# The beginning of a decoder step: weights staged in idle tiles, one weight split on another engine, small products between the first steps

## The chip, the cores and the metric

The kernel runs on one core of a Trainium2 chip. The metric is the device time of one execution in microseconds (us); lower is better. The engines are named as in the profile: PE (TensorE, the matrix products), DVE (VectorE), ACT (ScalarE), POOL (GpSimd) and SP (SyncE, which here only issues transfers).

## The reference, cut to what matters

One inference step of a decoder with two layers, for 512 prompt rows and 8 single-token samples, all float32, 1024 features wide. Only the first sublayer, windowed attention, is touched by the change:

```python
def qkv_proj(x, w_qkv, b_qkv, offset):
    qkv = x @ w_qkv + b_qkv
    q = qkv[..., :nq].reshape(B, T, N_HEADS, HEAD_DIM)
    k = qkv[..., nq:nq + nk].reshape(B, T, N_KV_HEADS, HEAD_DIM)
    v = qkv[..., nq + nk:].reshape(B, T, N_KV_HEADS, HEAD_DIM)
    return rope(q, pos), rope(k, pos), v
...
scores = jnp.einsum('bnqkgd,bnskd->bnkgqs', qb, kk) * ATTN_SCALE
probs = sink_softmax(scores, mask, sink)
o = jnp.einsum('bnkgqs,bnskd->bnqkgd', probs, vv) @ w_o
x = layer_norm(ALPHA * x + o)
```

After it come a gated feed-forward sublayer with a short convolution, then gated linear attention with four heads (a matrix state that is carried along the rows, and one more state for each sample), and a second feed-forward sublayer. Caches, states and the last convolution rows are outputs too.

## The kernel before, in words

**Rows and groups.** Activations lie with the features on the 128 partitions, as 8 chunks of 128 features (KD = 8). The rows are in two groups: a (256 prompt rows) and b (the other 256 and the 8 samples, 264 columns). A name ending in _a or _b belongs to that group.

**Products in three parts.** A float32 product is made from float32r products: every operand is split into a high part (a copy to float32r: wh of a weight, xh of x) and a low part (the rest: wl, xl), and three products are added up in one bank of PSUM: wh x xh, wh x xl, wl x xh. In group a, xh and xl lie in one tile, xs_a. `product` (L224) does this for one *unit*, a weight of 1024 x 128: 8 steps over the feature chunks, 24 matmuls; L236, L238 and L240 are the three products of a step. Where its flag `behind` (L230) is set, all eight wl products come after the others.

**Units.** Unit 0 gives the keys (`attn_k`, L575), unit 1 the values (`attn_v`), units 2 to 9 the queries of two heads each (`attn_q`, L610). Each is used twice, for group a and then for group b, three units later at the start (LAG - 1).

**Loading a weight** (`load_unit`, L180). SP's queue brings the weight into a tile `raw`, of which there are two (RAWS = 2); ACT (L194) or, for the units below HIACT, POOL (L196) makes wh, and DVE makes wl (L200). Six pairs of wh and wl are held (WSLOTS = 6). A transfer into `raw` waits until DVE has read what lay there two units earlier, and everything behind it on SP's queue waits too.

**The beginning** (`attn_open`, L514). PE first multiplies a tile of ones with itself, 8 times (L524 to L526; WARM = 8), into a bank that nobody reads. SP's queue, whose order is written out by hand, brings: unit 0 and x of group a in alternating pieces, unit 1 in four pieces, parameters, rope table and identity, unit 2 in two pieces, unit 3 in one, x of group b (x_b) in two pieces, the rest of the tables, and units 4 and 5. Group b's x is split by ACT (L313, xh_b) and DVE (L314, xl_b).

**Keys.** After unit 0, `rope` (L561) turns the keys with ACT, DVE and POOL into rr, and `attn_k` splits them: four copies by ACT (khi, L583 and L584) and four differences by DVE (klo, L586 and L587), since each half is kept on both halves of the partitions. The scores (L650, L651) take khi, klo and the queries' parts qs, which travel from the tile hl by small transfers (L622).

**Caches.** The samples' key and value caches, kc and vc, are two tiles of 128 x 1024. Transfers fill them late, while group b's queries are made (L631, L633).

**What sets the order.** Python code emits the work unit by unit, interleaving groups, with later parts of a head's work put on a list with a delay. From this a scheduler with a timing model of its own orders each engine's instructions, before the program is built; `issue_after(x)` keeps what follows behind instruction x, and only SP's queue at the beginning is fixed. So an edit at the beginning may reorder instructions much later.

**Linear attention**, which the prediction also speaks of: in each head the samples' states are updated on DVE from a tile vb (L1185) that a transfer fills for two samples at a time; only one vb exists. A gate tile sg is multiplied out of a PSUM bank (L1210), attm is a masked copy (L1073), dmn belongs to the next head's decay (L1025), and three transposes (L1090 to L1092) go into the bank that sg has been read from.

Of the kernel before, what the change touches and what calls it, by code (L numbers as in the profile page):

```python
# [11 lines left out]
F32 = mybir.dt.float32  # L12
F32R = mybir.dt.float32r
I32 = mybir.dt.int32
AF = mybir.ActivationFunctionType
ALU = mybir.AluOpType
# [4 lines left out]
P = 128  # L21
D = 1024
KD = 8
SEQ = 512
NS = 8
# [15 lines left out]
LAG = 4  # L41
# [1 line left out]

WSLOTS = 6
RAWS = 2
HIACT = 2

PAIRED = 4
ORDERED = 3
# [11 lines left out]
LOWS = 7  # L61
# [24 lines left out]
def in_turn(rows):  # L86

    return rows.rearrange("p t j -> p j t")
# [10 lines left out]
class Net:  # L99
# [77 lines left out]
        return self.acc.tile([P, 2, 512], F32, name=f"widep{i}")  # L177


    def load_unit(self, u, pieces=1, late=False):  # L180
        src, nt = self.units[u][0], self.units[u][1]
        nc = self.nc
        if nt == 0:
            return self.load_rank(u)
        r = self.raw.tile([P, KD * P], F32, name="raw")
        h, l = ((self.wx if u == self.extra else self.wts).tile([P, KD * P], F32R, name=name) for name in ("wh", "wl"))
        n = nt * P // pieces
        for c in (slice(i * n, (i + 1) * n) for i in range(pieces)):
            nc.sync.dma_start(out=r[:, c], in_=src[:, c])
            if late:  # L190
                self.spawn(self.parts(u, h[:, c], l[:, c], r[:, c], src[:, c]), 1)
                continue
            if u >= HIACT:
                nc.scalar.activation(h[:, c], r[:, c], AF.Copy)  # L194
            else:
                nc.gpsimd.tensor_scalar(h[:, c], r[:, c], 1.0, 0.0, op0=ALU.mult, op1=ALU.add)  # L196
            if self.units[u][2] in (self.ffn_down2, self.ffn_gate, self.ffn_value):
                self.low_by_dma(l[:, c], h[:, c], src[:, c])
            else:
                nc.vector.tensor_tensor(l[:, c], r[:, c], h[:, c].bitcast(F32), op=ALU.subtract)  # L200
        self.w[u] = (h, l)
# [22 lines left out]
    def product(self, g, u, rh, rl):  # L224
        nc = self.nc
        h, l = self.w[u]
        nt = self.units[u][1]

        tail = u in self.phases[2::3] or g.i and u in self.phases[2:4]
        behind = self.units[u][2] == self.ffn_down and g.i == 0 or g.i == 0 and nt == KD and not tail and any(e < u < e + LOWS for e in (*self.phases[2:4], *self.phases[5:6]))  # L230
        ps = self.acc.tile([P, 512], F32, name="accp")
        o = ps[:, :g.n].rearrange("p (j t) -> p j t", t=2)
        for k in range(nt):
            ks = slice(k * P, (k + 1) * P)
            xh, xl = in_turn(rh[:, k]), in_turn(rl[:, k])
            nc.tensor.matmul(o, h[:, ks], xh, start=k == 0, stop=False)  # L236
            if not tail:
                nc.tensor.matmul(o, h[:, ks], xl, start=False, stop=False)  # L238
            if not behind:
                nc.tensor.matmul(o, l[:, ks], xh, start=False, stop=not tail and k == nt - 1)  # L240
        for k in range(nt) if tail or behind else ():
            w, r = (h, rl) if tail else (l, rh)
            nc.tensor.matmul(o, w[:, k * P:(k + 1) * P], in_turn(r[:, k]), start=False, stop=k == nt - 1)
        self.final = self.nc.cur_bb.bb.instructions[-1]
        return ps[:, :g.n]
# [268 lines left out]
    def attn_open(self):  # L514
        nc, I = self.nc, self.I
        self.ap, self.ap_cm = self.open("attn")
        p = self.ap
        t = lambda s, name, dt=F32: p.tile(s, dt, name=name)
        self.rope_t = t([P, 2, NT], "rope_t")
        self.mask0 = t([P, P], "mask0")  # L520
        self.own = t([P, 2, P], "own", I32)


        warm = self.acc.tile([P, 512], F32, name="accp")  # L524
        for _ in range(WARM):
            nc.tensor.matmul(warm[:, :P], self.ones_a, self.ones_a, start=True, stop=True)  # L526
        with self.tc.manual_schedule(engines={mybir.EngineType.SP}):
            r = self.raw.tile([P, KD * P], F32, name="raw")
            h, l = (self.wts.tile([P, KD * P], F32R, name=n) for n in ("wh", "wl"))
            for m in range(0, KD, 4):  # L530
                c = slice(m * P, m * P + 4 * P)
                nc.sync.dma_start(out=r[:, c], in_=I["w_qkv"][0][:, c])
                nc.gpsimd.tensor_scalar(h[:, c], r[:, c], 1.0, 0.0, op0=ALU.mult, op1=ALU.add)
                self.load_x(0, m, m + 2)
                nc.vector.tensor_tensor(l[:, c], r[:, c], h[:, c].bitcast(F32), op=ALU.subtract)
                self.load_x(0, m + 2, m + 4)
            self.w[0] = (h, l)
            self.load_unit(1, 4)
            nc.sync.dma_start(out=self.par, in_=I["par"])
            nc.sync.dma_start(out=self.rope_t[:, :, 0:256], in_=I["rope"][:, :, 0:256])  # L540
            nc.sync.dma_start(out=self.ident, in_=I["ident"])
            self.load_unit(2, 2)
            self.load_unit(3)
            for m in range(0, KD, 4):
                self.load_x(1, m, m + 4)
            nc.sync.dma_start(out=self.rope_t[:, :, 256:], in_=I["rope"][:, :, 256:])
            nc.sync.dma_start(out=self.mask0, in_=I["mask"])
            nc.sync.dma_start(out=self.own, in_=I["own"])
            for i in range(4, WSLOTS):
                self.load_unit(i)  # L550
        self.bq = t([P, KD], "bq")
        nc.vector.tensor_scalar(self.bq, self.par[:, C_BQKV + 2:C_BQKV + 10], 0.125, None, op0=ALU.mult)
        self.khi = [t([P, SEQ], f"khi{v}", F32R) for v in range(2)]
        self.klo = [t([P, SEQ], f"klo{v}", F32R) for v in range(2)]
        self.vtok = t([P, 4, P], "vtok")
        self.kc = t([P, NS, P], "kc")
        self.vc = t([P, NS, P], "vc")
        self.qz = t([P, NS * P], "qz")
        nc.gpsimd.memset(self.qz, 0.0)

# [14 lines left out]
    def attn_k(self, g, u):  # L575
        nc = self.nc
        ps = self.product(g, u, g.xh, g.xl)
        r = self.rope(g, ps, 1.0, self.par[:, C_BQKV:C_BQKV + 1])
        cs = slice(g.c0, g.c0 + 256)
        for v in range(2):  # L580
            own = slice(64 * v, 64 * v + 64)
            oth = slice(64 - 64 * v, 128 - 64 * v)
            nc.scalar.activation(self.khi[v][own, cs], r[own, :256], AF.Copy)  # L583
            nc.scalar.activation(self.khi[v][oth, cs], r[own, :256], AF.Copy)  # L584
            hi = self.khi[v][own, cs].bitcast(F32)
            nc.vector.tensor_tensor(self.klo[v][own, cs], r[own, :256], hi, op=ALU.subtract)  # L586
            nc.vector.tensor_tensor(self.klo[v][oth, cs], r[own, :256], hi, op=ALU.subtract)  # L587
        yield 0
        if g.i:
            self.pcopy(self.kc[:, :, 127], r[:, 256:])  # L590
            nc.scalar.dma_start(out=self.O["k_prompt"], in_=r[:, 128:256])
# [901 lines left out]
```

## Time and profile before

| | |
|---|---|
| median of 3 executions | 1099.32 us (1099.08 to 1100.93) |
| the profiled execution's time, and its span | 1098.55 us, 1096.6 us |
| busy, share of the span: PE, DVE, ACT, POOL | 97%, 80%, 60%, 28% |
| PE busy in the first three stretches of 10 us | 8.06, 8.97, 9.58 us |
| PE's granted clock there | 0.89, 0.94, 1.00 |
| DVE busy there | 4.89, 9.26, 9.27 us |
| ACT busy there | 4.32, 7.10, 4.89 us |
| transfers there | 256, 300, 146 GB/s |

The profile is one execution seen by the hardware profiler. A row of its timeline has the start, the duration, the engine, the line, the operation, what is written and read (`out<-in`), shape, type and count, and in brackets the idle time before it with what ended it. A row of stretches has from:to, the length, each engine's busy time with its number of instructions in brackets, and last the granted clock of PE (1.00 is full speed), the busy share of the transfer engines and GB/s. Groups of rows that follow each other closely are merged into one with a count. Some records of matmuls can be missing.

### The profile page before, as it was taken

What the parts mean: (1) busy time and instruction counts of PE and PEld (TensorE: products, weight loads), DVE (VectorE), ACT (ScalarE), POOL (GpSimd) and SP (SyncE); (2) the same over time, 40 slices, a digit from 0 to 9 for tenths busy, and PEclk for the clock granted to TensorE, in tenths of its full rate; (3) what the DMA queues carried; (4) which work ended last, traced back from release to release, by engine and by line L of the source; (5) the groups of instructions that cost most, each with busy time, mean ns of one, the idle gap of its engine ahead of it and who ended that gap; (6) DMA issues with size and microseconds to landing.
All of it is one profiled execution on the core that took longest, in us unless ns stands there. A gap on an engine that the chain in (4) does not pass through costs nothing.

```text
span 1096.6 us, 23781 instructions
## 1 busy us (share of the span) xinstructions
PE 1058.9 (97%) x9174; PEld 1031.2 (94%) x9174; DVE 882.0 (80%) x1797; ACT 663.1 (60%) x1308; POOL 303.1 (28%) x512
## 2 busy tenths in 40 slices
PE   8999999999999999999899999999999999999996
PEld 8997899999999999999799899899999999999995
DVE  7897668988778878978667678778988788888975
ACT  5677667766655665547545456458776655655643
POOL 4576562221111110274111100362221111110163
PEclk9999999999999999999999999999999999999998
DMA  7554048587777774437224364558588777774412
GB/s 233 147 173 125 21 128 207 135 215 191 180 177 178 176 174 116 124 130 204 66 74 145 115 185 136 164 170 215 134 205 197 180 174 177 175 185 116 116 66 79
DMA packets 65472, 167.44 MB, mean 153 GB/s; under 512 B 8104, under 2 KB 28624, under 8 KB 65360
## 3 DMA queue, kind: packets, MB, share of 16 engines
q1 hardware_dynamic: 50960, 119.47, 33.8%
q0 software_dynamic: 12240, 44.57, 23.1%
q10 hardware_dynamic: 2160, 1.89, 0.5%
q8 instruction: 72, 1.18, 0.4%
q14 instruction: 40, 0.33, 0.1%
HBM read 153.24 MB, written 8.47 MB: 147 GB/s over the span
## 4 chain that ended last, share of the span: by engine, by line
PE 66%; DVE 13%; DMA 10%; ACT 5%; issue 5%; SPq 1%; POOL 0%; DVEq 0%; ACTq 0%; POOLq 0%
PE widep L308 8%; PE widep L310 8%; PE widep L309 8%; PE accp L236 6%; PE accp L238 6%; PE accp L240 6%; PE widep L921 5%; PE widep L920 5%; PE widep L919 5%; DMA vb<-dv 2%; DMA wl<-in_w_up 2%; DVE wl L200 2%; PE onep L310 1%; PE onep L309 1%; PE onep L308 1%
## 5 line engine op out<-in xcount | busy, mean ns | idle before, releaser
L313 ACT ACTIVATE wh<-raw 128x1024 fp32r<-128x1024 f32 x72 | 76.2, 1061 | 98.7 <-PE widep L920 57.3
L194 ACT ACTIVATE wh<-raw 128x1024 fp32r<-128x1024 f32 (+1 forms) x92 | 96.0, 1047 | 52.3 <-PE accp L238 19.4
L309 PE MATMUL widep<-tl,wh 128*128 128x264 f32 (+1 forms) x432 | 119.1, 276 | 0.0
L310 PE MATMUL widep<-th,wl 128*128 128x264 f32 (+1 forms) x432 | 119.1, 276 | 0.0
L308 PE MATMUL widep<-th,wh 128*128 128x264 f32 (+1 forms) x432 | 119.1, 276 | 0.0
L236 PE MATMUL accp<-xh_b,wh 128*128 128x264 f32 x400 | 113.1, 283 | 2.6 <-DVE hprod L817 2.6
L240 PE MATMUL accp<-xh_b,wl 128*128 128x264 f32 x400 | 111.5, 279 | 0.0
L236 PE MATMUL accp<-xs_a,wh 128*128 128x256 f32 x400 | 106.1, 285 | 5.4 <-DVE sg L1202 2.5
L238 PE MATMUL accp<-xl_b,wh 128*128 128x264 f32 x384 | 107.5, 280 | 0.0
L206 POOL DMA_DIRECT2D wl<-in_w_down x28 | 24.3, 866 | 293.6 <-ACT wl L205 271.0
L238 PE MATMUL accp<-xs_a,wh 128*128 128x256 f32 x384 | 103.1, 284 | 0.5
L314 DVE TENSOR_TENSOR wl<-raw,wh 128x1024 fp32r<-128x1024 f32 x72 | 87.5, 1218 | 7.5 <-ACT wh L313 7.5
L205 ACT ACTIVATE wl<-wh 128x1024 fp32r<-128x1024 f32 x85 | 89.1, 1051 | 1.0
L200 DVE TENSOR_TENSOR wl<-raw,wh 128x1024 fp32r<-128x1024 f32 (+2 forms) x64 | 79.0, 1244 | 12.3 <-ACT wh L194 11.5
L236 PEld LDWEIGHTS accp<-xs_a,wh 128*128 128x128 f32 x400 | 76.7, 195 | 7.0 <-DVE sg L1202 2.9
L308 PEld LDWEIGHTS widep<-th,wh 128*128 128x128 f32 x432 | 82.1, 190 | 0.0
L309 PEld LDWEIGHTS widep<-tl,wh 128*128 128x128 f32 x432 | 82.1, 190 | 0.0
L310 PEld LDWEIGHTS widep<-th,wl 128*128 128x128 f32 x432 | 82.1, 190 | 0.0
L236 PEld LDWEIGHTS accp<-xh_b,wh 128*128 128x128 f32 x400 | 75.7, 189 | 4.3 <-DVE hprod L817 3.4
L308 PE MATMUL widep<-xh_b,wh 128*128 128x264 f32 x288 | 79.6, 276 | 0.0
L309 PE MATMUL widep<-xl_b,wh 128*128 128x264 f32 x288 | 79.5, 276 | 0.0
L310 PE MATMUL widep<-xh_b,wl 128*128 128x264 f32 x288 | 79.5, 276 | 0.0
(419 smaller groups left out, 4113.1 us busy)
## 6 DMA issues: line engine op xcount, KB each, us to landing
raw<-in_w_up SPq DMA_DIRECT2D x88, 512.0 KB, 4.0
wl<-in_w_up POOLq DMA_DIRECT2D x52, 512.0 KB, 7.1
raw<-in_w_down SPq DMA_DIRECT2D x44, 512.0 KB, 3.9
wl<-in_w_down POOLq DMA_DIRECT2D x28, 512.0 KB, 6.5
raw<-in_w_gla SPq DMA_DIRECT2D x24, 512.0 KB, 3.5
raw<-in_w_mix_o SPq DMA_DIRECT2D x16, 512.0 KB, 4.1
qs<-hl SPq DMA_DIRECT2D x64, 64.0 KB, 2.1
sgla<-in_state_gla SPq DMA_DIRECT2D x16, 256.0 KB, 2.9
```

What stands on the lines that cost most here:

```text
L194: nc.scalar.activation(h[:, c], r[:, c], AF.Copy)
L200: nc.vector.tensor_tensor(l[:, c], r[:, c], h[:, c].bitcast(F32), op=ALU.subtract)
L205: self.nc.scalar.activation(l, h.bitcast(F32), AF.Copy, scale=-1.0)
L236: nc.tensor.matmul(o, h[:, ks], xh, start=k == 0, stop=False)
L238: nc.tensor.matmul(o, h[:, ks], xl, start=False, stop=False)
L240: nc.tensor.matmul(o, l[:, ks], xh, start=False, stop=not tail and k == nt - 1)
L308: self.nc.tensor.matmul(o, h[:, ks], rh, start=k == 0, stop=False)
L309: self.nc.tensor.matmul(o, h[:, ks], rl, start=False, stop=False)
L310: self.final = self.nc.tensor.matmul(o, l[:, ks], rh, start=False, stop=k == KD // 2 - 1).ins
L313: self.nc.scalar.activation(hi, src, AF.Copy)
L314: self.nc.vector.tensor_tensor(lo, src, hi.bitcast(F32), op=ALU.subtract)
L919: nc.tensor.matmul(o, h[:, ks], rh, start=k == 0, stop=False)
```

## The change

Five edits, all for the first 25 us of the program:

- Units 2 and 3 are loaded into the tiles kc and vc, which are allocated earlier for that, each in two pieces; they no longer take a `raw` tile.
- HIACT goes from 2 to 1: wh of unit 1 is made by ACT, not by POOL.
- In group a the wl products of units 0 to 3 come behind their other products (`u < LAG`).
- Between the first eight steps of unit 0 in group a stands one product of ones with ones, seven in all, into the bank of the opening products.
- khi and klo, of both groups, stay behind the last instruction of ACT and of DVE that has been emitted when x_b's splits have been.

```diff
-HIACT = 2
+HIACT = 1
...
-    def load_unit(self, u, pieces=1, late=False):
+    def load_unit(self, u, pieces=1, late=False, r=None):
...
-        r = self.raw.tile([P, KD * P], F32, name="raw")
+        if r is None:
+            r = self.raw.tile([P, KD * P], F32, name="raw")
...
-        behind = self.units[u][2] == self.ffn_down and g.i == 0 or g.i == 0 and nt == KD and not tail and any(e < u < e + LOWS for e in (*self.phases[2:4], *self.phases[5:6]))
+        behind = self.units[u][2] == self.ffn_down and g.i == 0 or g.i == 0 and nt == KD and not tail and (u < LAG or any(e < u < e + LOWS for e in (*self.phases[2:4], *self.phases[5:6])))
...
             if not tail:
-                nc.tensor.matmul(o, h[:, ks], xl, start=False, stop=False)
+                step = nc.tensor.matmul(o, h[:, ks], xl, start=False, stop=False)
+            if u == 0 and g.i == 0 and k < nt - 1:
+                with self.tc.issue_after(step.ins):
+                    nc.tensor.matmul(self.warm[:, :P], self.ones_a, self.ones_a, start=True, stop=True)
...
-            self.load_unit(2, 2)
-            self.load_unit(3)
+            self.load_unit(2, 2, r=self.kc.rearrange("p b d -> p (b d)"))
+            self.load_unit(3, 2, r=self.vc.rearrange("p b d -> p (b d)"))
             for m in range(0, KD, 4):
                 self.load_x(1, m, m + 4)
+            self.rows = [next(x for x in reversed(nc.cur_bb.bb.instructions) if x.engine == engine)
+                         for engine in (mybir.EngineType.Activation, mybir.EngineType.DVE)]
...
-        for v in range(2):
...
+        with self.tc.issue_after(self.rows[0]), self.tc.issue_after(self.rows[1]):
+            for v in range(2):
```

Lines of the changed kernel are up to five higher than before. What the scheduler makes of it on PE at the end of unit 0 (`accp_218` before and `accp_219` now are unit 0's bank, `accp_259` and `accp_267` unit 1's, `accp_102` that of the ones), before:

```order
L236 MATMUL accp_218<-xs_a_87,wh_112 128x256
L236 MATMUL accp_259<-xs_a_87,wh_141 128x256
L238 MATMUL accp_259<-xs_a_87,wh_141 128x256
L238 MATMUL accp_218<-xs_a_87,wh_112 128x256
L240 MATMUL accp_218<-xs_a_87,wl_113 128x256
```

and now:

```order
L239 MATMUL accp_219<-xs_a_87,wh_114 128x256
L242 MATMUL accp_102<-ones_a_80 128x128
L237 MATMUL accp_219<-xs_a_87,wh_114 128x256
L237 MATMUL accp_267<-xs_a_87,wh_143 128x256
L239 MATMUL accp_267<-xs_a_87,wh_143 128x256
L237 MATMUL accp_267<-xs_a_87,wh_143 128x256
L239 MATMUL accp_267<-xs_a_87,wh_143 128x256
L239 MATMUL accp_219<-xs_a_87,wh_114 128x256
L247 MATMUL accp_219<-xs_a_87,wl_115 128x256 x8
```

A product of ones follows each of the first seven steps, four matmuls of unit 1 are drawn ahead where two were, and unit 0's eight low products stand in one row at its end.

On ACT, from unit 2's high part to unit 5's (`raw`, `kc` and `vc` are where the weight lies; `bq` marks a query unit, `par` keys or values), before:

```order
L194 ACTIVATE wh<-raw 128x512 x2
L597 ACTIVATE ra<-accp,par 128x256
L583 ACTIVATE khi_209<-rr 64x256
L584 ACTIVATE khi_209<-rr 64x256
L583 ACTIVATE khi_210<-rr 64x256
L584 ACTIVATE khi_210<-rr 64x256
L194 ACTIVATE wh<-raw 128x1024
L313 ACTIVATE xh_b<-x_b 128x264 x4
L566 ACTIVATE ra<-accp,bq 128x256
L313 ACTIVATE xh_b<-x_b 128x264 x4
L566 ACTIVATE ra<-accp,bq 128x256
L194 ACTIVATE wh<-raw 128x1024 x2
```

and now, from unit 3's second half on:

```order
L195 ACTIVATE wh<-vc 128x512
L317 ACTIVATE xh_b<-x_b 128x264 x4
L570 ACTIVATE ra<-accp,bq 128x256
L317 ACTIVATE xh_b<-x_b 128x264 x4
L588 ACTIVATE khi_212<-rr 64x256
L589 ACTIVATE khi_212<-rr 64x256
L588 ACTIVATE khi_213<-rr 64x256
L589 ACTIVATE khi_213<-rr 64x256
L570 ACTIVATE ra<-accp,bq 128x256
L195 ACTIVATE wh<-raw 128x1024
L622 ACTIVATE hl<-rr 128x256
L195 ACTIVATE wh<-raw 128x1024
```

The four khi copies moved from ahead of unit 3's high part to behind x_b's splits, ahead of the high parts of units 4 and 5, and one hl copy came in between these two.

The scheduler also reorders the rest of attention and the linear attention; in the two feed-forward sublayers the order of PE's matmuls is as it was. One place in the first linear-attention head, on DVE, where the last pair of samples is updated (L1185, now L1190), before:

```order
L1185 SCALAR_TENSOR_TENSOR sgla<-vb,kraw,sgla 128x256 x2
L1210 SCALAR_TENSOR_TENSOR sg<-tp,par,sg 128x256
L1073 COPY_PREDICATED attm_7292<-causal,sc 128x256
L1025 TENSOR_SCALAR dmn<-sc,par 128x264
L314 TENSOR_TENSOR hs_a<-sg,hs_a 128x2x128
```

and now:

```order
L1190 SCALAR_TENSOR_TENSOR sgla<-vb,kraw,sgla 128x256 x2
L1078 COPY_PREDICATED attm_7300<-causal,sc 128x256
L1030 TENSOR_SCALAR dmn<-sc,par 128x264
L1215 SCALAR_TENSOR_TENSOR sg<-tp,par,sg 128x256
L318 TENSOR_TENSOR hs_a<-sg,hs_a 128x2x128
```

The two instructions attm and dmn moved ahead of sg; PE's transposes into sg's bank come behind sg in both.

More of the change, by code (lines that the diff above doesn't have):

```diff
@@ L521, in attn_open @@
         self.own = t([P, 2, P], "own", I32)
-        warm = self.acc.tile([P, 512], F32, name="accp")
+        self.kc = t([P, NS, P], "kc")
+        self.vc = t([P, NS, P], "vc")
+        self.warm = self.acc.tile([P, 512], F32, name="accp")
         for _ in range(WARM):
-            nc.tensor.matmul(warm[:, :P], self.ones_a, self.ones_a, start=True, stop=True)
+            nc.tensor.matmul(self.warm[:, :P], self.ones_a, self.ones_a, start=True, stop=True)
         with self.tc.manual_schedule(engines={mybir.EngineType.SP}):
@@ L555, in attn_open @@
         self.vtok = t([P, 4, P], "vtok")
-        self.kc = t([P, NS, P], "kc")
-        self.vc = t([P, NS, P], "vc")
         self.qz = t([P, NS * P], "qz")
@@ L579, in attn_k @@
         cs = slice(g.c0, g.c0 + 256)
-        for v in range(2):
[L581 to L587, printed above, removed]
+        with self.tc.issue_after(self.rows[0]), self.tc.issue_after(self.rows[1]):
+            for v in range(2):
+                own = slice(64 * v, 64 * v + 64)
+                oth = slice(64 - 64 * v, 128 - 64 * v)
+                nc.scalar.activation(self.khi[v][own, cs], r[own, :256], AF.Copy)
+                nc.scalar.activation(self.khi[v][oth, cs], r[own, :256], AF.Copy)
+                hi = self.khi[v][own, cs].bitcast(F32)
+                nc.vector.tensor_tensor(self.klo[v][own, cs], r[own, :256], hi, op=ALU.subtract)
+                nc.vector.tensor_tensor(self.klo[v][oth, cs], r[own, :256], hi, op=ALU.subtract)
         yield 0
```

## The prediction

> **What bounds the kernel now.** I read the page first, then TensorE's waits, then the first 26 us of each engine's timeline, and last TensorE's granted clock in single stretches.
>
> ```profile
> span 1096.6 us, 23781 instructions
> PE 1058.9 (97%) x9174; PEld 1031.2 (94%) x9174; DVE 882.0 (80%) x1797; ACT 663.1 (60%) x1308; POOL 303.1 (28%) x512
> ```
>
> TensorE is busy for 97% of the span. The change leaves its real work as it is and adds seven small products, so it can only gain where TensorE waits or runs slowly. The profiled execution took 1098.55 us, 1.95 more than its span; the median of the runs shown is 1099.32, so I subtract from 1099.3. About 0.2% (2.2 us) is what a measurement can tell from no change.
>
> ```profile
> 11.54 0.28 PE L236 MATMUL accp<-xs_a,wh 128*128 128x256 f32 x1
> ...
> 13.99 0.28 PE L238 MATMUL accp<-xs_a,wh 128*128 128x256 f32 x1
> ```
>
> From the first of these rows to the last are 22 steps in 2.45 us: 0.111 us is the slot of a matmul at full clock. Each row's 0.28 is longer, since matmuls overlap.
>
> ```profile
> 4.42:7.84 3.42, 2.57 (x14) 1.00 1.01 342
> 7.84:11.25 3.41, 3.40 (x15) 0.50 1.01 320
> ...
> 540.32:543.73 3.41, 0.88 (x7) 1.00 0.00 0
> ...
> 605.17:608.58 3.41, 1.67 (x15) 1.00 0.82 273
> ```
>
> These are TensorE's stretches: length, busy time (instructions), granted clock. The clock halves at 7.84 for 3.41 us, after a stretch with 14 instructions. It halves again at 543.73, after one with 7. The falls are 535.89 us apart, 157 times 3.413, so stretches of that length look like a grid. The one from 605.17, on the same grid, had 15 instructions and full clock after it. In slots, 14 of 31 fell and 15 held. A fall costs half of 3.41 us: 1.7.
>
> The Trainium skill ("TensorE: Matmul & The Clock Gate", section "Why this matters for your kernels") asks only that idle gaps stay below about 3 us. Ahead of the first fall the idle time was 0.85 us in all (3.42 - 2.57), so here the trace disagrees, and the row decides. By the page's rule the added products would be pure cost, and the forecast about 1099.3.
>
> **The change part by part.** The start of TensorE:
>
> ```profile
> 1.07 3.64 PE L526 MATMUL accp<-ones_a 128*128 128x128 f32 x16 [1.07 <-POOL ones_a L117]
> ...
> 8.64 0.58 PE L238 MATMUL accp<-xs_a,wh 128*128 128x256 f32 x1
> ...
> 11.31 0.39 PE L240 MATMUL accp<-xs_a,wl 128*128 128x256 f32 x2
> ...
> 17.66 0.38 PE L236 MATMUL accp<-xs_a,wh 128*128 128x256 f32 x1 [0.48 <-ACT wh L194]
> ...
> 18.92 0.38 PE L240 MATMUL accp<-xs_a,wl 128*128 128x256 f32 x1 [0.55 <-DVE wl L200]
> ...
> 21.48 0.28 PE L238 MATMUL accp<-xl_b,wh 128*128 128x264 f32 x1
> ...
> 25.20 0.28 PE L236 MATMUL accp<-xh_b,wh 128*128 128x264 f32 x1
> ```
>
> ```profile
> 539.60 0.59 PE L1115 MATMUL pv<-sp,q_a 128*128 128x256 f32 x2
> 540.03 0.59 PE L1118 MATMUL pv<-vk,attm 128*128 128x256 f32 x2
> ```
>
> *Ones between steps, low products behind.* The eight opening products took 3.64 us, 0.455 each. A float32 product of 256 columns later takes 0.43 from one row to the next, so one of 128 columns takes 0.215 at full clock, two slots; the opening ran at half pace, whatever its clock column says. With a little for the weights I take 0.23. In the stretch to 7.84 three low products leave and three ones enter: 14 - 3 + 6 = 17 slots, above the 15 that held. So I take the clock to hold. From the matmul at 8.64 (it waits for VectorE's fifth low part, unchanged) there follow, with it, 19 matmuls and 3 ones to the end of the first product, four of them the second unit's: 19 x 0.111 + 3 x 0.23 = 2.80, so 11.44. Before, that product's last slot ended at 11.42: the ones eat here what the clock gives. Gained is what comes next.
>
> *Second weight's high part on ScalarE.*
>
> ```profile
> 8.63 2.17 POOL L196 TENSOR_SCALAR wh<-raw 128x256 fp32r<-128x256 f32 x4 [1.25 <-DMA raw<-in_w_qkv]
> ```
> ```profile
> 7.46 1.51 ACT L313 ACTIVATE xs_a<-x_a 128x256 fp32r<-128x256 f32 x4 [0.69 <-DMA x_a<-in_x]
> 11.63 0.47 ACT L566 ACTIVATE ra<-accp,par 128x256 f32<-128x256 f32 x1 [2.65 <-PE accp L240]
> ```
>
> Four pieces of 2.17 us leave GpSimd; on ScalarE four of this size took 1.51, in a hole of 2.65 us. They end near 10.6 and TensorE wants them at 11.4: nothing, or 1.5 if that hole were gone.
>
> *Third and fourth weight in the caches' tiles.*
>
> ```profile
> 8.28 3.88 SPq L189 DMA_DIRECT2D raw<-in_w_qkv  x3
> 12.21 0.99 SPq L509 DMA_DIRECT2D x_b<-in_x  x2
> ```
> ```profile
> 11.40:13.20 1.80, 1.80 (x18) 1.80 (x17) 1.43 (x7) 1.51 (x3) 0.53 (x1) 1.00 0.35 58
> 13.20:18.00 4.80, 4.32 (x37) 3.93 (x35) 4.42 (x8) 3.59 (x8) 1.49 (x2) 1.00 0.99 346
> ```
>
> The fourth weight waited for a raw buffer, and with it everything behind it on SP's queue, the second rows' x included: 58 GB/s for 1.8 us where 346 followed. That is (346 - 58) / 346 x 1.8 = 1.5 us of transfers, and x_b comes so much earlier. The later loads into those tiles are the caches', far behind: no cost.
>
> *Keys' parts behind the rows' splits.*
>
> ```profile
> 14.80 0.42 ACT L583 ACTIVATE khi<-rr 64x256 fp32r<-64x256 f32 x1 [0.24 <-POOL rr L572]
> ...
> 17.51 1.46 ACT L313 ACTIVATE xh_b<-x_b 128x264 fp32r<-128x264 f32 x4
> 18.88 0.46 ACT L566 ACTIVATE ra<-accp,bq 128x256 f32<-128x256 f32 x1
> 19.24 1.62 ACT L313 ACTIVATE xh_b<-x_b 128x264 fp32r<-128x264 f32 x4
> ...
> 22.11 1.05 ACT L194 ACTIVATE wh<-raw 128x1024 fp32r<-128x1024 f32 x1
> ...
> 24.73 0.40 ACT L617 ACTIVATE hl<-rr 128x256 fp32r<-128x256 f32 x1
> ```
>
> Four khi copies (1.72 us) stood ahead of the fourth weight's high part, for which TensorE waited to 17.66. They go, and with them the waits at 17.66 and 18.92. From 11.44 on TensorE has 20 + 24 + 24 matmuls to the end of the fourth unit, 7.55, and two transposes, about 0.25: 19.24, against 21.37 before (the slot ahead of the row at 21.48). That is 2.1 earlier. Then the first unit for the second rows, 24 matmuls, to 21.9.
>
> What is late next: the fifth and sixth weights' high parts, now behind khi on ScalarE. From x_b's landing, 15.5 (its split at 17.51 may have followed other work; 16.0 at the latest), ScalarE has 1.46 + 0.46 + 1.62 + 1.72 + 0.47 + 1.05 + 0.40 + 1.05 = 8.2 to the sixth weight: 23.8. TensorE stands idle for about 1.4 us there and begins the second unit's second rows near 24.05, against 25.20: 1.15 gained. If x_b lands at 16.0 it is 0.65. If the scheduler's queue never lets ScalarE be last, TensorE's own work (21.9 plus four slots) gives 2.8. I take 1.0, near the queue's value, with a little off because the first scores need VectorE's low parts, which the new order brings forward less than ScalarE's.
>
> Whether the lead is kept is read from TensorE's waits, summed by who ended them (total, times, longest), first from 30 to 60 us and then from 60 to 140, the longest of each:
>
> ```profile
> PE sc L650 <- ACT pr L667: 0.3, 1, 0.3
> ```
> ```profile
> PE sc L650 <- ACT pr L667: 1.6, 3, 0.7
> ```
>
> TensorE waits so little that no other engine sets the pace there; an engine that did would have it waiting. A lead passes through, and the short waits of the second stretch can move by some tenths either way with the new order. In the up and down projections the order of TensorE's products is the old one. Sum: 1099.3 - 1.0 = 1098.3.
>
> **The rivals.**
>
> *The clock falls at the start all the same.* For it: 17 slots against a bound known only as 14 to 15, of records of which some may be missing, and a float32 product need not count as two slots. Against it: they run from 5.4 us on in places where TensorE had stood idle. Then from 8.64 on a matmul costs 0.21 and a one 0.455 until 11.25; the first product ends at 12.7, 1.27 later, and ScalarE's queue behind it ends at 24.8: gain 0.1, 1099.2.
>
> *The second fall goes as well.*
>
> ```profile
> 543.16 0.38 PE L236 MATMUL accp<-xs_a,wh 128*128 128x256 f32 x1 [2.53 <-DVE sg L1202]
> ```
>
> This wait lay in one stretch. Moved earlier by g it is cut by the border at 540.32, and the second stretch keeps 0.57 + g of work; 15 slots are 1.67, so g of 1.1 would save another 1.7: 1099.3 - 1.1 - 1.7 = 1096.5. It needs the grid to lie the same in every execution. The Trainium skill (same page, section "What's actually happening") says the window runs freely and does not restart with a kernel. The 157 whole steps agree within one execution; between executions no run here shows it, and by the page this gain would be chance.
>
> *Slower: VectorE's order in the linear-attention heads.*
>
> ```profile
> 605.74 0.28 PE L240 MATMUL accp<-xh_b,wl 128*128 128x264 f32 x1
> 607.75 0.33 PE L1090 MATMUL tp<-ident,k_b 128*128 128x128 f32 x1 [1.74 <-DVE sg L1210]
> ```
> ```profile
> 606.42 0.88 DVE L1185 SCALAR_TENSOR_TENSOR sgla<-vb,kraw,sgla 128x256 f32<-128x256 f32 x2 [3.17 <-DMA vb<-dv]
> 607.22 0.48 DVE L1210 SCALAR_TENSOR_TENSOR sg<-tp,par,sg 128x256 f32<-128x256 f32 x1
> 607.62 0.43 DVE L1073 COPY_PREDICATED attm<-causal,sc 128x256 f32<-128x256 int32 x1
> 607.94 0.48 DVE L1025 TENSOR_SCALAR dmn<-sc,par 128x264 f32<-128x264 f32 x1
> ```
>
> VectorE waits for vb, and sg, which frees TensorE's bank, stands right behind. In the new order attm and dmn come between: 0.8 later, less three matmuls that TensorE now has ahead of its wait (0.3). From the row at 605.74 to the one at 607.75 TensorE now waits 1.9; that grows by 0.5 and leaves that stretch some 10 slots, so the clock falls: 0.5 + 1.7 = 2.2, 1100.5 with the start's gain. If a second head goes the same way, 1102.7, slower. Against it: the vb chain may itself run earlier.
>
> **How the numbers follow.** Forecast 0.38 (own range 1096.5 to 1099); clock falls at the start 0.12; second fall gone 0.26; one head 0.14; two heads 0.10. Faster by over 0.2% (below 1097.1): 0.26 and 0.06 from the forecast's long end, 0.32. Slower (above 1101.5): two heads, and 0.04 of one head without the start's gain, 0.14. Within: 0.54. Range: from the second fall gone with 0.7 more at the start, 1095.8, to one head without the start's gain, 1101.4.
>
> **What would show it.** Right: granted clock 1.00 from 7.8 to 11.3, the first q-unit load without a gap at 12 us, no wait of TensorE near 17 to 19, one of 1 to 1.5 us near 22 to 24 for wh by ScalarE, and the second unit's second rows begun near 24. Wrong: a clock of 0.50 after 7.8; that beginning later than 25; or a second half-clock stretch near 607.

## The result, and the profile after

The changed kernel takes 1112.2 us (median of 6, 1110.0 to 1113.9), against 1099.3 for the kernel before beside it (6 runs, 1096.8 to 1102.2). The ratio is 1.0108, 95% interval 1.0092 to 1.0123: slower by 11.9 us by the ratio and by 12.9 by the medians, where 1098.3 us was forecast. Its profiled execution took 1110.02 us. From its page:

```profile
span 1108.1 us, 23806 instructions
PE 1063.5 (96%) x9188; PEld 1034.3 (93%) x9188; DVE 883.1 (80%) x1798; ACT 664.0 (60%) x1313; POOL 296.0 (27%) x508
```

The span grew by 11.5 us and PE's busy time by 4.6: the larger part is waiting, and the busy time has grown by more than seven small products (1.5 us), as a slow clock would do. The beginning, by stretches of the clock's grid (busy time of PE, PEld, DVE, ACT, POOL with the instructions in brackets, granted clock, transfer share, GB/s):

```profile
4.97:8.38 3.41, 2.69 (x15) 1.92 (x16) 2.20 (x6) 1.37 (x5) 0.62 (x1) 1.00 1.03 336
8.38:11.80 3.42, 3.19 (x28) 3.00 (x28) 3.06 (x10) 2.23 (x7) 0.60 (x1) 1.00 0.98 320
11.40:13.20 1.80, 1.80 (x19) 1.80 (x18) 0.53 (x4) 0.99 (x2) 0.00 (x0) 1.00 1.01 325
...
22.04:25.45 3.41, 1.99 (x12) 1.41 (x11) 3.33 (x8) 3.30 (x6) 0.92 (x2) 1.00 0.05 14
25.45:28.86 3.41, 3.41 (x18) 3.41 (x17) 3.41 (x4) 0.42 (x1) 1.99 (x2) 0.50 0.56 178
```

The clock holds through 8 us, the transfers have no hole at 12 us, and a new half-clock stretch lies at 25.45, after one with 12 matmuls. What PE does around it:

```profile
11.07 1.06 PE L247 MATMUL accp<-xs_a,wl 128*128 128x256 f32 x8
11.96 0.28 PE L237 MATMUL accp<-xs_a,wh 128*128 128x256 f32 x1
...
19.89 0.28 PE L237 MATMUL accp<-xh_b,wh 128*128 128x264 f32 x1
...
23.79 0.38 PE L237 MATMUL accp<-xs_a,wh 128*128 128x256 f32 x1 [0.39 <-ACT wh L195]
...
25.04 0.38 PE L237 MATMUL accp<-xs_a,wh 128*128 128x256 f32 x1 [0.76 <-ACT wh L195]
...
25.37 0.35 PE L237 MATMUL accp<-xh_b,wh 128*128 128x264 f32 x1
```

The rest is found by setting the same matmul (line, tiles, rank) of two traces side by side. This is how much later than in the trace of before it starts, the median over the 6 us from each of these times of before; runs named below stand beside the changed kernel. Up to 90 us single products of one such window lie 2 us and more apart, since the order is new:

| us later at | 30 | 60 | 90 | 140 | 300 | 555 | 690 | 780 | 1080 |
|---|---|---|---|---|---|---|---|---|---|
| changed kernel | 1.7 | 0.7 | 2.4 | 6.7 | 5.8 | 3.9 | 5.1 | 10.9 | 11.2 |
| low products alone | 1.1 | 0.4 | 3.3 | 7.9 | 8.0 | 5.6 | 7.6 | 11.6 | 11.3 |
| without the ones | -0.2 | 0.0 | 2.9 | 3.8 | 3.8 | 4.2 | 4.7 | 6.2 | 6.0 |
| five ones alone | 0.7 | 0.8 | 1.2 | 4.1 | 2.1 | 0.5 | 0.8 | 3.6 | 3.3 |
| seven ones alone | 1.4 | 1.2 | 2.3 | 7.8 | 7.9 | 8.1 | 8.2 | 10.4 | 11.3 |
| seven ones, other bank | 1.2 | 0.9 | 2.1 | 1.1 | -0.7 | -0.7 | -0.9 | 2.1 | 5.6 |

Each half-clock stretch is 1.7 in such a row. The changed kernel loses in two places, both far from the edits: the end of attention (100 to 140 us) and the end of the linear attention with the out-projection and the feed-forward start behind it (640 to 780). PE and the others there, before and then after:

```profile
60.00:142.00 82.00, 76.43 (x695) 68.05 (x695) 64.37 (x194) 55.83 (x199) 50.50 (x97) 1.00 0.32 94
640.00:790.00 150.00, 145.97 (x1237) 139.72 (x1236) 120.22 (x268) 92.24 (x198) 44.77 (x72) 1.00 0.61 168
```
```profile
60.00:142.00 82.00, 73.67 (x655) 65.14 (x656) 63.00 (x191) 53.42 (x196) 47.11 (x96) 0.98 0.32 93
640.00:790.00 150.00, 140.34 (x1172) 132.96 (x1171) 112.52 (x252) 85.50 (x186) 40.89 (x64) 1.00 0.58 160
```

PE idles 8.3 us instead of 5.6 in the first and 9.7 instead of 4.0 in the second, and has a lower clock in the first. Its waits after the change, from 60 to 140 us and from 640 to 790:

```profile
PE tp L684 <- ACT pt L686: 2.0, 3, 1.0
PE sc L655 <- ACT pr L672: 1.4, 2, 1.1
PE pv L735 <- DVE hl_b L318: 1.0, 1, 1.0
PE pv L703 <- POOL pu L690: 1.0, 2, 0.5
```
```profile
PE accp L247 <- DMA wl<-in_w_up: 2.9, 3, 1.3
PE accp L237 <- ACT hh_b L317: 1.5, 1, 1.5
PE tp L379 <- DVE s_a L371: 1.3, 1, 1.3
PE tp L1095 <- DVE sg L1215: 1.3, 1, 1.3
```

Before, the longest from 640 to 790 us were these:

```profile
PE accp L236 <- DVE hprod L817: 1.4, 2, 1.0
PE accp L236 <- ACT hh_b L313: 0.8, 1, 0.8
```

No work was added in either place. What changed there is the order that the scheduler wrote.

### The profile page after: what moved, and what is told of

Same layout as the page of the kernel before. It is cut to its first block, busy times and chain, and to the rows that moved or that the text cites. A ratio compares the mean times of both kernels' runs of the same rounds, so it can differ in the third digit from the quotient of the medians.

```text
span 1108.1 us, 23806 instructions
## 1 busy us (share of the span) xinstructions
PE 1063.5 (96%) x9188; PEld 1034.3 (93%) x9188; DVE 883.1 (80%) x1798; ACT 664.0 (60%) x1313; POOL 296.0 (27%) x508
## 4 chain that ended last, share of the span: by engine, by line
PE 64%; DVE 14%; DMA 9%; ACT 6%; issue 4%; POOL 1%; SPq 1%; DVEq 0%; ACTq 0%; POOLq 0%
PE widep L312 8%; PE widep L313 8%; PE widep L314 8%; PE accp L237 5%; PE accp L239 5%; PE widep L926 5%; PE widep L924 5%; PE widep L925 5%; PE accp L244 4%; DMA vb<-dv 3%; DMA wl<-in_w_up 2%; DVE wl L201 2%; DVE de L1205 1%; PE onep L313 1%; PE onep L314 1%
## 5 line engine op out<-in xcount | busy, mean ns | idle before, releaser
L237 PE MATMUL accp<-xs_a,wh 128*128 128x256 f32 x400 | 104.0, 281 | 5.6 <-ACT wh L195 2.6
L239 PE MATMUL accp<-xs_a,wh 128*128 128x256 f32 x384 | 100.9, 280 | 0.5 <-DVE xs_a L318 0.2
L201 DVE TENSOR_TENSOR wl<-raw,wh 128x1024 fp32r<-128x1024 f32 (+1 forms) x61 | 74.8, 1234 | 14.1 <-ACT wh L195 13.1
L849 DVE TENSOR_TENSOR merged<-widep,conv 128x528 f32<-128x528 f32 x72 | 37.4, 561 | 53.8 <-PE widep L314 53.6
```

The costliest lines, as they stand in the source:

```text
L239: step = nc.tensor.matmul(o, h[:, ks], xl, start=False, stop=False)
```

## The experiments

Single executions of one kernel differ by some us (before ran from 1095.5 to 1106.1 in all its runs), so verdicts rest on the ratio to runs of before on the same chip; 0.1% is 1.1 us. Theory A: the later order costs, whatever edit brought it about. Rival B: the beginning costs, and the rest follows from a late start. Theory C: it is chance, and the median stays within 2 us of before.

**One edit alone, or one undone.** Low products alone:

```diff
-... and not tail and any(e < u < e + LOWS ...)
+... and not tail and (u < LAG or any(e < u < e + LOWS ...))
```

> The kernel before with one edit alone: the low products of units 0 to 3 behind the others, for group a. The beginning's loads, splits and ones are those of before, but the scheduler then writes attention and the linear attention nearly as in the changed kernel. Theory A (the later orders cost: some 5 us at the end of attention, where the changed kernel's lead of -1.5 turned to -6.7, and 6.6 us from the linear attention to the second out-projection, where the lag went from 4.3 at 550 us to 10.9 at 782): 1099.3 + 5 + 6.6 less the half-clock stretch at 543 that may go, so 1107 to 1111. Theory B (the lost time comes from the beginning: the wait for wh at 23 to 25 us, the half-clock stretch at 25.45 and what follows from a later start): 1098 to 1101, as this kernel has none of it. Theory C (chance: the clock's grid lies otherwise in each execution): single executions spread over several times 1.7 us, and the median stays within 2 us of before.

1108.7, ratio 1.0080 [1.0061, 1.0098]. Nothing of the beginning's transfers, splits or ones is in it, and the row in the table is nearly that of the changed kernel. B falls, and so does C. Then the changed kernel without the ones, and without the low products' move:

```diff
-            if u == 0 and g.i == 0 and k < nt - 1:
-                with self.tc.issue_after(step.ins):
-                    nc.tensor.matmul(self.warm[:, :P], self.ones_a, self.ones_a, start=True, stop=True)
```

> The changed kernel without the seven products of ones; all else of the beginning as changed. The scheduler's order from 550 us on is then that of before on DVE, ACT and SP, and on PE but for two rows; attention's order is a third one. Theory A: the 6.6 us between 550 and 782 us come back, so 1112.2 - 6.6 = 1105.6, less or more by what the third attention order does (up to 5 either way), and plus up to 1.7 if the clock halves at the start. Theory B: nothing comes back, the beginning still loses its lead near 23 to 25 us and the clock may halve at 8 as well: 1112 to 1114.

```diff
-... and (u < LAG or any(e < u < e + LOWS ...))
+... and any(e < u < e + LOWS ...)
```

> The changed kernel with the low products of units 0 to 3 back in their steps; all else as changed. The scheduler's order from 550 us on is that of before on DVE, ACT and SP. Theory A: 1112.2 - 6.6 = 1105.6, up to 5 either way with attention's order, as for the run without ones. Theory B: 1112 to 1113.

1102.3, ratio 1.0011 [0.9992, 1.0030], and 1103.0, 1.0040 [1.0024, 1.0057]. To take away seven products of 0.2 us returns nine tenths of the loss. The keys' parts alone, `issue_after(self.rows[...])` added to the kernel before:

> The kernel before with the keys' parts (khi, klo) behind the rows' splits, and nothing else. The order from 550 us on is that of before. Theory A: no cost after 550 us; attention's order is new, so 1099.3 with 0 to 5 more by what its end does: 1099 to 1104. Theory B (the fifth and sixth weights' high parts come late at 23 to 25 us): the wait at 17.7 goes and that one comes, with a half-clock stretch behind it: 1100 to 1101, all of it made before 30 us.

1103.6, 1.0032 [1.0016, 1.0048]. Theory A had room for it (1099 to 1104), B had not (1100 to 1101, all of it made before 30 us): the trace is 1.0 later at 30 us and 3.6 at 140.

**The later order by itself.** A few products of ones among the samples' value products at attention's end flip the order behind 550 us, by their number: three do, four don't, and in the changed kernel the other way round.

```diff
             nc.tensor.matmul(pv[:, b * 16:(b + 1) * 16], self.vc[:, b], ...)
+            if b in (1, 3, 5):          # four: (0, 2, 4, 6)
+                nc.tensor.matmul(pv[:, 256:384], self.ones_a, self.ones_a, start=True, stop=True)
```

> The kernel before with three products of ones among the eight products of the samples' probabilities with the value cache, in a part of their bank that nobody reads. Attention and all before 550 us keep the order of before (but for 19 rows on PE); from 550 us on the scheduler writes the order of the changed kernel. So this is the beginning of before with the later order of the changed kernel. Theory A (that order by itself costs about 4 us: the lag grew by 7.0 and 6.0 us from 555 to 786 us in the two kernels that have it, by 2.0 to 3.8 in the three that have the order of before): 1100.3 + 0.7 for the ones + 4 = 1105. Rival D (the order in the linear attention is harmless; what is lost there follows from an attention that ends late): 1101. Clock: TensorE's fall near 138 us was not there before, so the ones can save nothing.

> The same with four products of ones: here the order from 550 us on stays that of before (4 rows on PE, 1 on POOL differ). Theory A and rival D alike: 1100.3 + 0.9 = 1101.2. The difference to the run with three ones is the later order alone, less 0.2 for a product of ones: 4 by theory A, 0 by rival D.

> The changed kernel with three products of ones among the samples' value products: attention keeps its order but for 3 rows, and from 550 us on the scheduler writes the order of before. Theory A: 1112.2 + 0.7 - 4 = 1109 from the later order; and less 1.7 or 3.4 if the clock no longer halves near 138 us. Theory E on that (the clock halves after a stretch of 3.41 us in which TensorE streams less than about 1.36 us of columns, however long its instructions are busy; the samples' products of 16 columns take 0.11 to 0.22 us each and stream 0.03 per pair; the stretch ahead of the fall had 1.03, the lowest stretches that held had 1.36): three ones add 0.67, so no fall near 138, and 1105.5 to 1107. Rival to E (idle time decides): the falls stay, 1109. Rival D: 1112.2 + 0.7 - up to 3.4.

> The changed kernel with four such products of ones: attention as in the changed kernel but for 4 rows, and from 550 us on the order of the changed kernel nearly (40 rows on PE). Theory A: 1112.2 + 0.9, less 3.4 if the falls near 138 us go (theory E): 1109.7; 4 more than with three ones. Rival D: as with three ones.

On the kernel before: 1103.7 with the new later order (1.0041 [1.0025, 1.0057]), 1101.5 with the old one (1.0021 [1.0008, 1.0035]). On the changed kernel: 1106.6 with the old (1.0075 [1.0059, 1.0092]), 1110.4 with the new (1.0105 [1.0089, 1.0122]). So the later order costs 0.20 and 0.30%, 2 to 3.5 us, a little less than the 4 of theory A; rival D (harmless) falls. The traces say the same: from 640 to 780 us the six with the new later order fall 5.3 to 8.1 us further behind the trace of before, the thirteen others 2.0 to 4.5. So only a part of the time lost there is the order's price; before's own trace was quick at that place. The waits from 640 to 790 us of the changed kernel with the old later order no longer have the low parts of w_up at their head:

```profile
PE tp L1097 <- DVE sg L1217: 1.4, 1, 1.4
PE accp L237 <- DVE hprod L824: 1.0, 2, 0.7
...
PE accp L244 <- DMA wl<-in_w_up: 0.2, 1, 0.2
```

Theory E was half wrong: the clock halves near 136 us in all four traces (from 135.75 to 137.99), so three or four ones are no remedy there. That 1106.6 lies where E had it (1105.5 to 1107) is luck, since the falls that it took away are still there. Its measure held (last section).

**One link of the later wait.** In the new order POOL's first product of the convolution states waits for their load, and the low parts' transfers stand behind it on POOL's queue:

```profile
L775 POOL TENSOR_TENSOR base<-sconv,par x1: 492/492/492, 744.5 to 744.5; 128x176 f32<-128x176 f32 x1
...
  DMA sconv<-in_state_conv: 2.9, 1
```

```diff
-        nc.scalar.dma_start(out=self.sconv, in_=self.I["state_conv"][layer])
+        if layer == 0:
+            nc.scalar.dma_start(out=self.sconv, in_=self.I["state_conv"][layer])
+        else:
+            nc.gpsimd.memset(self.sconv, 0.0)
```

> The changed kernel, whose second feed-forward sublayer fills its convolution states with zeros by POOL instead of loading them (this leaves that load out); all orders as in the changed kernel but for a few rows on ACT and POOL. Theory H (the load lands after 4.2 us, where it took 2.2 in the order of before; POOL's first product of the states stands waiting for it for 2.9 us, and the low parts of the first up-projection weights, by POOL's queue, and the layer norm's sums start late behind it; TensorE waits 2.9 us for wl and 1.3 for s_a): POOL's wait goes, TensorE's wait for wl falls below 1, and the lag grows from 730 to 786 us by 0 to 1 instead of 2.5: 1110. Rival I (the low parts are late by their own transfers of 5 to 12 us): the waits stay, 1112.

This kernel leaves out the load of the second layer's convolution states. POOL's wait went and PE's for wl fell from 2.9 to 1.6 in the trace (theory H had it below 1). But that trace is of the quickest execution, 1107.7, and the median of 4 is 1113.8, ratio 1.0121 [1.0095, 1.0146], above both H (1110) and rival I (1112). The wait is real, but its price doesn't show in the time; which waits make up the 2 to 3.5 us stays open.

**The beginning.** The changed kernel with the keys' parts behind the fifth and sixth weights as well (`self.rows` taken after that loop), and the same without the low products' move:

> The changed kernel with the keys' parts held behind the fifth and sixth weights' parts as well (and the order of before from 550 us on). Theory F (of the beginning: the ones keep the clock up, TensorE arrives early at the second rows, and there waits for the fifth and sixth weights' high parts behind the keys' parts on ACT; this wait and the halving of the clock after it at 25.45 eat the gain): the wait for wh by ACT at 23 to 25 us goes, no half-clock stretch near 25, and at 30 us the lag against before is -1 to 0 where the changed kernel had 1.7. Rival G (the second rows' parts or the transfers are late there anyway, and the wait only changes its name): lag at 30 us still 1 to 1.7. In time: 1106.6, as with the order of before from 550 us on in the changed kernel, less 0.7 for the three ones there, less 2 by F: 1104; 1106 by G; attention's new order may add or take 2.

> As the run with the keys' parts behind the fifth and sixth weights, and with the low products of units 0 to 3 back in their steps. The order from 550 us on is that of before. Of the runs so far the one without the low products' move had attention's best course (lag 1.7 at 140 us, with a half-clock stretch at 25.8 in it). Theory F: that stretch goes, so 1103.0 - 1.7 - some tenths: 1100 to 1101.5. Rival G: 1103.

1106.3, 1.0071 [1.0048, 1.0093], and 1107.4, 1.0070 [1.0049, 1.0091]. In the first, PE at 30 us is 1.0 ahead of before (F), though a wait of the next operand takes the place of that for wh (G's name for it). Later a head's scores wait at 92.30 for the queries' parts, and the clock halves at 94.89:

```profile
PE accp L244 <- DVE wl L201: 1.5, 1, 1.5
PE sc L655 <- DMA qs<-hl: 1.1, 1, 1.1
```

At 90 us it is 3.0 behind, up to 1.7 of it from that half-clock stretch. A lead at 30 us was worth nothing at 90, and the time is G's (1106), not F's (1104). The second is 0.1 late at 30 us, 4.3 at 90, and misses both theories by 4 us and more.

**Ones, by their number.** Ones alone in the kernel before, behind all seven steps, behind five, behind six:

```diff
+            if u == 0 and g.i == 0 and k < nt - 1:      # five: k < 5, six: k < 6
+                with self.tc.issue_after(step.ins):
+                    nc.tensor.matmul(self.warm[:, :P], self.ones_a, self.ones_a, start=True, stop=True)
```

> The kernel before with the seven products of ones alone. The order from 550 us on is that of before, attention's is a new one. Clock by theory E (columns streamed in a stretch decide): it holds at the start, as in the two runs with ones (the four runs without them lost it); the first product ends as early as there. Then the waits of before at 17.7 and 18.9 us take the gain: lag at 30 us 0 (within 0.5), and 1100 to 1103 with attention's new order. If the clock falls at the start: lag at 30 us about 1.2.

> The kernel before with five products of ones, behind the first five steps of unit 0; the order is that of before (5 rows on PE differ, none on DVE or ACT). Theory A: the clock holds at the start and the first product ends some 1 us earlier, the waits for wh and wl at 17 to 19 us take it; 1099 to 1100.5. Rival K: 1106 to 1108, in the way of the run with seven ones alone, 1110.

> The kernel before with six such products; from here on the scheduler writes attention anew, as for seven (7 rows on PE between six and seven, 876 between six and five). Theory A: 1108 to 1111, near the seven's 1110; so some 9 us for one product of ones of 0.2 us. Rival K: within 1 of the run with five.

Seven: 1110.0, 1.0104 [1.0085, 1.0123]. Five: 1103.4, 1.0020 [1.0006, 1.0034]. Six: 1108.5, 1.0058 [1.0038, 1.0077]. Five leave the order as it was but for 5 rows; the sixth makes the scheduler write attention anew, and costs 0.38%, about 4 us where 9 were expected, for a product of 0.2. My forecast of 1100 to 1103 for seven missed the price of the new order by 7.

**Edits with the order kept.** HIACT = 1, units 2 and 3 in kc and vc (unit 3 in one piece), five ones; then the same with `u in (2, 3)` for the low products:

> As many of the change's edits as leave the scheduler's order as it was before: unit 1's high part by ACT, units 2 and 3 in the caches' tiles (unit 3 in one piece), five products of ones; without the low products' move and the keys' move. From attention on the order is that of before (29 rows on PE differ, all at the beginning, 3 on DVE). Theory A (the edits are harmless or a small gain, and what is lost is made by the order that the scheduler writes after them): 1098.5 to 1100, the median of before being 1099.8; the lag at 140 us then within 1 of that at 30 us, but for half-clock stretches near 136, which before has in some executions too. Rival K (the edits themselves cost, by more transfers early or by the ones): 1102 or more.

> As the first of these, and with the low products of units 2 and 3 behind the others; the order stays that of before (75 rows on PE, all at the beginning). Theory A: within 1 of the first of these, 1098.5 to 1100. Rival K, and any theory by which the low products' move itself costs (it cost 8.4 us alone, for units 0 to 3): 1102 or more.

1102.9, 1.0018 [1.0004, 1.0031], and 1102.9, 1.0012 [0.9996, 1.0028]. In microseconds both lie where rival K had them (1102 or more), but the kernel before took 1101.4 beside them. By the ratio most of the edits cost 0.1 to 0.2% without the new orders, far from the 1.08%; a small gain, which theory A allowed (1098.5 to 1100), does not show either.

**What attention's new order costs by.** The seven ones alone, at the end of attention:

```profile
134.70 0.39 PE L701 MATMUL pv<-pu,vtok 128*64 128x128 f32 x4
138.21 3.19 PE L733 MATMUL pv<-pts,vc 128*128 128x16 f32 x16 [3.12 <-DVE hl_b L317]
141.94 0.59 PE L236 MATMUL accp<-hh_b,wh 128*128 128x264 f32 x1 [0.54 <-ACT hh_b L737]
```

Before, the same two came as follows, with out-projection products between:

```profile
128.56 0.39 PE L698 MATMUL pv<-pu,vtok 128*64 128x128 f32 x4
...
132.02 1.86 PE L730 MATMUL pv<-pts,vc 128*128 128x16 f32 x16
```

There is one bank pv. In the new order the samples' value products stand right behind a head's, and PE waits until ACT and DVE have read that one out. ACT itself comes to it late, behind work of group a's layer norm (L358) that waits for POOL:

```profile
136.21 0.42 ACT L358 ACTIVATE sq<-x_a 128x256 f32<-128x256 f32 x1 [1.87 <-POOL s_a L371]
...
137.33 0.37 ACT L316 ACTIVATE hh_b<-pv 128x256 fp32r<-128x256 f32 x1
```

The clock then halves for two stretches:

```profile
135.27:138.68 3.41, 0.47 (x4) 1.00 0.01 2
138.68:142.10 3.42, 2.88 (x15) 0.50 0.00 0
142.10:145.51 3.41, 3.41 (x22) 0.50 0.00 0
```

The last two runs give these products another bank, of the scores in the kernel with seven ones, of the transposes in the changed kernel:

```diff
-        pv = self.mtile("pv")
+        pv = self.mtile("sc")          # changed kernel: "tp"
```

> The kernel with seven products of ones alone, and the samples' value products in a bank of the scores instead of the heads' value bank, of which there is one. The scheduler puts them before the out-projection's products and the last heads' value products instead of behind both; else the order is as with seven ones (40 rows on PE, 8 on DVE, all at attention's end). Theory M (at attention's end the new order sets the samples' products behind a head's in the same bank; TensorE waits 3.1 us until DVE has read that head out, everything of group b waits with it, and the clock halves for 6.8 us): the wait goes, and one or both half-clock stretches: 1110 - 3.1 - 1.7 to 3.4, 1103.5 to 1105. Rival N (the chain through ACT and DVE to the last heads is as long anyway, another wait of that length takes its place): 1109 to 1110.

> The changed kernel with the samples' value products in the transposes' bank; the order is its own but for 10 rows on PE at attention's end, and from 550 us on exactly its own. Theory M: the wait of 1.0 us for DVE's reading of the bank goes and with it up to 3.4 us of half clock near 138: 1112.2 - 1.0 - 0 to 3.4, 1108 to 1111. Rival N: 1112.

1104.1, 1.0028 [1.0013, 1.0042], and 1109.0, 1.0068 [1.0044, 1.0093]. Both lie where theory M had them. How much the bank was worth is less sure. Seven ones had 1.0104, but on another chip; six ones, with 7 rows of PE different, had 1.0058 on this one. So it is 0.30 to 0.76% (3 to 8 us), and why six and seven differ is not shown. The changed kernel had 1.0108, so there it is 0.40% (4 us), with intervals that just touch; rival N falls clearly for the first kernel alone. The scheduler also moves these products with their bank (40 rows of PE in the first, 10 in the second), so bank and place changed together. With seven ones, PE now does them early, and the wait that is left is shorter, with no half clock there:

```profile
129.33 1.86 PE L733 MATMUL sc<-pts,vc 128*128 128x16 f32 x16
...
138.57 0.44 PE L701 MATMUL pv<-pl,vtok 128*64 128x128 f32 x4 [1.03 <-DVE hl_b L317]
```

At 140 us this trace is 6.7 us ahead of that with seven ones (7.8 and 1.1 in the table), about the wait and the two half-clock stretches (3.1 + 3.4). In the changed kernel with the other bank the wait of 1.0 is gone, but granted clock is 0.50 from 137.34 to 144.17, as long as before the move, and 1.4 us is gained at 140.

The Trainium skill (Perfetto Trace Analysis, section "Matmuls") advises to rotate independent groups of matmuls through different banks, so that one is read out while the next is multiplied; these two runs agree, by 3 to 8 and by some 4 us.

None of these kernels beats the kernel before.

## Why the prediction was wrong, point by point

**The step that failed** is "A lead passes through, and the short waits of the second stretch can move by some tenths either way with the new order." I read from before's trace that PE hardly waits between 30 and 140 us and took that as a property of the work. It was a property of that order. The text itself had said that attention and the linear attention are reordered, and priced the first at some tenths, the second at one or two heads' sg. Measured in the changed kernel: 0.20 to 0.30% for the later order, about 0.4% for the one bank at attention's end, and the rest of the 1.08% from the beginning and from other waits in attention that no run separates. The gain of 1.0 at the start did not show in the time either: with the order kept, most of the edits cost 0.1 to 0.2%.

**The lead itself** came out as 1.7 behind at 30 us, not the 1.0 ahead that I took. Four other profiles share this beginning: 1.4 behind in the one whose clock also halves near 25 us, 0.1 to 1.0 ahead in the three where it doesn't.
- *Clock at the start*: right, it held, and did so in all 12 profiles with five or more ones where full clock came by 7 us; without, it fell in 3 of 5. The reason given, slots, was the wrong measure. The first product's end was forecast for 11.44; its last slot ends at 11.96, with a wait of 0.23 for DVE's low part still in it.
- *ACT's split of unit 1*: nothing, as forecast.
- *Transfers*: the hole went (325 GB/s where there were 58), but x_b was not 1.5 us earlier. It was issued at 10.40 instead of 12.21, and from the views of transfers, before and after, its time to landing grew from 6.2 to 7.9, so that its second piece landed at 18.7 where it had at 18.9:

```profile
x_b<-in_x SPq DMA_DIRECT2D x2, 528.0 KB, 6.2
```
```profile
x_b<-in_x SPq DMA_DIRECT2D x2, 528.0 KB, 7.9
```

Its first split begins at 17.27 instead of 17.51:

```profile
17.27 1.63 ACT L317 ACTIVATE xh_b<-x_b 128x264 fp32r<-128x264 f32 x4 [0.68 <-DMA x_b<-in_x]
```

The bytes that filled the hole belong to what had been issued around it, the tables and weights too (281 GB/s over the first 17.2 us where 262 were). Here, at a transfer share of 1.0, the earlier issue was not an earlier landing.
- *Waits at 17.66 and 18.92*: gone, as forecast; the fourth unit ends at 19.89 (19.24 forecast).
- *What is late next*: right in kind, the fifth and sixth weights' high parts, 0.39 + 0.76 = 1.15 us of waiting (1.4 forecast), but the second unit's second rows begin at 25.37 instead of 24.05, as x_b was late. And the forecast held no fall of the clock against its own wait. By its slots 1.4 us of idle time leave 18 in a stretch of 3.41, above the 15 that held. But around waits PE does less than its busy time says: this stretch was busy for 1.99 us, 18 slots, and had 12 matmuls. The clock halved at 25.45, a price of 1.7.

**The rivals.** That the clock falls at the start all the same is out. The fall at 543 us was gone in this trace, and 1.2 us with it, but others of these kernels have it at 531 to 552: chance, as its condition said. The slower rival had the side right and the place wrong: the wait for sg near 606 us, 1.7 in before, is not in the trace after, and between 555 and 640 us nothing is lost (3.9 behind, then 3.3). The loss comes later, from 640 to 780 us.

**The chances.** 0.14 for slower, all of it on one named mechanism. A scheduler that rewrites this much deserved far more, in both directions (side by side, some 940 of PE's 9,100 products stand out of the common order of the two traces), and the range ended at 1101.4 for lack of that term.

## What to carry to other kernels

Where a scheduler writes the order, an edit's price has two terms, the edit and the new order, and the second can be the larger by far (here 4 us for a product of 0.2): look at what the new order does to single buffers (who stands right behind whom in one bank) before counting microseconds at the edit. To separate the two, vary the edit until the order stays (five ones instead of six), or flip the order with an edit that does nothing. A lead at the start is worth only what no later wait absorbs, and every wait that you forecast also has to be held against the clock.

## What the runs showed of the hardware

**What the clock counts.** Busy time is not it. The stretch that halved the clock near 138 us in the changed kernel:

```profile
134.68:138.09 3.41, 2.15 (x26) 1.91 (x26) 1.60 (x3) 1.17 (x3) 3.41 (x7) 1.00 0.02 5
138.09:141.50 3.41, 2.87 (x17) 2.50 (x18) 1.11 (x4) 1.16 (x4) 2.15 (x7) 0.50 0.00 0
141.50:144.92 3.42, 3.42 (x23) 3.09 (x21) 0.61 (x2) 0.38 (x1) 0.00 (x0) 0.50 0.20 53
```

It had 26 instructions and was busy for 2.15 us, and the clock fell; another stretch of before was busy for 1.67 us with 15 and kept it. The first is made of half-width products and of products of 16 columns. If each record counts for the columns that it streams (0.111 us per 256 columns, a float32 record twice that, half width half), the traces fall apart cleanly. Over the 20 profiles some 6,300 stretches were at full clock: the 37 with up to 1.11 us streamed were all followed by half clock, of the 29 from there to 1.38 us 16 were, and of the others none (some records can be missing). The border is near 1.25 of 3.41 us. By this measure the stretch of the changed kernel had 1.03 and that of before at 605 us 1.59. At half clock the border is much the same: after every stretch with up to 1.35 us streamed the clock stayed down, as from 138.09 on (0.59), and after every one with 1.44 or more it came back.

**Where the grid lies.** Its borders stood anywhere from 0.01 to 3.26 us into a step of 3.41, counted from the first instruction, in these 20 executions. The Trainium skill (TensorE: Matmul & The Clock Gate, section "What's actually happening") calls the window free-running, and the traces agree. So what a weak place costs is in part chance. The end of attention had one to three half-clock stretches, 1.7 us each, in all 12 profiles with a new order and the old bank, and one or two in 3 of 6 with the order of before; of the two with another bank one had two and one none. The profiled execution of before, from which I forecast, was one of the lucky ones. Part of the spread of 10 us between single executions of one kernel may come from there; no run separates it.
